# An instance norm on one core: another dealing of row blocks to partitions, and direct emission of the hand-scheduled part

## The chip, the core and the metric

One core of a Trainium2 chip runs the whole kernel. The metric is the device time of one execution in microseconds (us), as a median over runs. TensorE is not used. The work is done by VectorE (DVE), ScalarE (ACT) and the core's sixteen DMA engines. SyncE (SP) only waits and issues transfers.

## What is computed

The input is a float32 array of 256 batches, 256 channels and 4096 positions, thus 65,536 rows of 4096 values. Each row is normalised by its own mean and variance:

```
mean = np.mean(x, axis=2, keepdims=True)
var = np.var(x, axis=2, keepdims=True)
return ((x - mean) / np.sqrt(var + eps)).astype(np.float32)
```

Every row is independent of every other, so any row may be worked on in any partition, as long as its result is written back to where it came from. The input holds 1073.7 MB and the output as much. Each byte is read once and written once.

## The kernel before

**Tiling.** The 65,536 rows are cut into 128 tiles of 512 consecutive rows (8 MB). `x_t` and `out_t` (lines 34 and 35) give the layout within a tile: partition p of the 128 holds the K = 4 consecutive rows 4p to 4p+3. Four rows of 4096 float32 values are 64 KB, which lie next to each other in HBM. So a tile is 128 blocks of 64 KB; partition p holds block p, and the blocks of neighbouring partitions are neighbours in HBM.

**Buffers.** Three SBUF buffers `X[0]` to `X[2]` of 128 x 4 x 4096 take the tiles in turn. A tile is normalised in place and stored from the same buffer.

**Work on a tile.** For each of the four rows in a partition, VectorE makes one pass that scales and sums (line 87). ScalarE then squares and sums the deviation from the mean (line 137) and takes the root (line 146). VectorE makes the reciprocal and the offset (lines 98 and 100). The final scaling is VectorE's (line 112) except for three quarters of the last row, which ScalarE does (line 151). Both engines run these as a loop over tiles written out for three buffers (lines 225 and 237), with a few tiles before and after.

**Transfers.** All loads and stores are issued by SyncE, on one queue, in an order written out by hand (lines 196 to 218). In the loop of line 208 each step is `store(t)` (line 165), then `load(t + 2)` (line 170). The store waits for the five done marks of its tile; the load waits for the store of tile t - 1, since it takes that buffer. Waits and clears are the helper `take` (lines 66 to 68). The first and the last tile move in two halves (lines 199 and 181), so that the compute starts and ends earlier. The function `rows_of` (line 155) picks a tile's rows in HBM, by a constant number outside the loop and by the loop's register inside it.

**Emission.** The three programs are written in `nc.Block()`, with one function for each engine (lines 193 to 246). At its end the block brings the engines together (line 193).

## Time and profile before

| what | value |
|---|---|
| median of ten runs | 4962.64 us (4961.6 to 4999.17; nine of them at or below 4963.14) |
| the profiled execution's own time | 4963.37 us |
| its span in the profile | 4961.2 us |
| DVE busy | 3297.8 us |
| ACT busy | 2407.6 us |
| HBM read, written | 1073.74 MB, 1073.74 MB |
| DMA issues | 259, of them 253 of 8 MB and 6 of 4 MB |

The profiled execution's time and its span differ by 2.2 us, which lie outside the span. A sum over the trace is a sum against 4961.2 us of span; the profiled execution lies 0.7 us above the median. Besides the groups of instructions, the trace has a record of each packet that a DMA engine moved (start, duration, bytes), without the engine's number. All but a few of these packets are one partition's share of a tile, 64 KB.

### The profile page before, as it was taken

To read this page: it belongs to the slowest core of one execution; us is meant where nothing else is said; L and a number is where in the kernel's file an instruction comes from. 1 tells how busy PE (TensorE), PEld (TensorE's weight loads), DVE (VectorE), ACT (ScalarE), POOL (GpSimd) and SP (SyncE) were. 2 spreads that over 40 slices of the span, in tenths; PEclk is the share of its full clock that TensorE was granted. 3 is DMA by queue.
4 is the path that set the end of the run, shared out by engine and by line. 5 is a ranking of instruction groups with operands and counts; after the bars stand their busy time and mean duration, and the time that the engine had idled before them with its cause. 6 is when DMAs were issued, how large, how long until landed. Compare 5 with 4: busy or idle time off the path is not lost.

```text
span 4961.2 us, 5954 instructions
## 1 busy us (share of the span) xinstructions
DVE 3297.8 (66%) x2049; ACT 2407.6 (49%) x1412; POOL 0.2 (0%) x4
## 2 busy tenths in 40 slices
DVE  6666666666666666666666666666666666666666
ACT  4455444554445544455445544455444554445544
POOL 0000000000000000000000000000000000000000
DMA  9999999999999999999999999999999999999999
GB/s 422 431 437 431 434 434 432 436 434 432 438 432 432 437 433 434 435 433 436 433 433 436 433 432 437 433 433 435 433 436 433 433 436 434 432 437 433 433 436 398
DMA packets 37298, 2147.52 MB, mean 433 GB/s; under 512 B 4144, under 2 KB 4144, under 8 KB 4144
## 3 DMA queue, kind: packets, MB, share of 16 engines
q1 hardware_dynamic: 37296, 2147.50, 100.0%
q14 instruction: 2, 0.02, 0.0%
HBM read 1073.74 MB, written 1073.74 MB: 433 GB/s over the span
## 4 chain that ended last, share of the span: by engine, by line
DVE 62%; another core or an unknown queue 31%; issue 4%; DMA 2%; ACT 0%; DVEq 0%; ACTq 0%; SPq 0%
DVE x L87 44%; DVE x L112 16%; DMA x<-in_x_dram 1%; DVE nbias L100 1%; DMA out_dram<-x 1%; DVE rstd L98 1%; ACT junk L137 0%; DVEq L68 0%; DVEq L225 0%; ACT L146 0%; ACT std L146 0%; DVEq L193 0%; ACTq L68 0%; ACTq L67 0%
## 5 line engine op out<-in xcount | busy, mean ns | idle before, releaser
L87 DVE TENSOR_SCALAR_CACHE_REDUCE x<-x 128x4096 f32<-128x4096 f32 x512 | 2232.3, 4416 | 1581.3 <-DMA x<-in_x_dram 1581.3
L137 ACT ACTIVATE junk<-x,mean 128x4096 f32<-128x4096 f32 x512 | 1883.1, 3678 | 2368.2 <-DVE x L87 2368.2
L112 DVE TENSOR_SCALAR x<-x,rstd,nbias 128x4096 f32<-128x4096 f32 (+1 forms) x512 | 1004.1, 2003 | 33.9 <-DVE nbias L100 29.3
L151 ACT ACTIVATE x<-x,nbias,rstd 128x3072 f32<-128x3072 f32 x130 | 383.1, 2947 | 146.0 <-DVEq L68 146.0
L137 ACT ACTIVATION_READ_ACCUMULATOR junk<-x,mean 128x1 f32 x512 | 95.5, 186 | 0.0
L146 ACT ACTIVATE std<-ss,eps_tile 128x2 f32<-128x2 f32 x256 | 75.6, 295 | 19.1
L98 DVE RECIPROCAL rstd<-std 128x2 f32<-128x2 f32 x256 | 40.6, 158 | 19.4 <-ACT std L146 19.4
L100 DVE SCALAR_TENSOR_TENSOR nbias<-mean,rstd 128x2 f32<-128x2 f32 x256 | 41.0, 160 | 8.9
L87 DVE DVE_READ_ACCUMULATOR x<-x 128x1 f32 x512 | 42.3, 83 | 0.0
L137 ACT ACT_TABLE_LOAD x1 | 1.3, 1283 | 1.2 <-DVE eps_tile L222 1.2
L146 ACT ACT_TABLE_LOAD x1 | 1.3, 1283 | 0.1
L222 DVE MEMSET eps_tile<- 128x1 f32 x1 | 0.1, 59 | 1.0 <-SPq L192 1.0
L259 POOL MEMSET const-bfloat16-1.0<- 128x1 bf16 x1 | 0.1, 101 | 0.0
L259 POOL MEMSET const-uint8-127<- 128x1 uint8 x1 | 0.1, 101 | 0.0
L259 POOL MEMSET const-float32-0.0<- 128x1 f32 x1 | 0.1, 99 | 0.2 <-issue 0.2
L259 POOL MEMSET const-float32-1.0<- 128x1 f32 x1 | 0.1, 98 | 0.0
## 6 DMA issues: line engine op xcount, KB each, us to landing
out_dram<-x SPq DMA_DIRECT2D x4, 4096.0 KB, 19.5
x<-in_x_dram SPq DMA_DIRECT2D x2, 4096.0 KB, 16.7
x<-in_x_dram SPq DMA_DIRECT2D x127, 50.3
out_dram<-x SPq DMA_DIRECT2D x126, 31.6
```

The source lines that it names most:

```text
L87: V.tensor_scalar(out=x[:, r, :], in0=x[:, r, :], scalar1=1.0 / d, scalar2=None, op0=ALU.mult, op1=ALU.add, accum_out=mean[s][:, r : r + 1 ...
L98: mine(V.reciprocal(out=rstd[s][:, c], in_=std[s][:, c]))
L100: mine(V.scalar_tensor_tensor(out=nbias[s][:, c], in0=mean[s][:, c], scalar=-1.0 / d, in1=rstd[s][:, c], op0=ALU.mult, op1=ALU.mult))
L112: V.tensor_scalar(out=x[:, r, f], in0=x[:, r, f], scalar1=rstd[s][:, c], scalar2=nbias[s][:, c], op0=ALU.mult, op1=ALU.add,).then_inc(dn, 1)
L137: mine(A.activation(out=junk, in_=x[:, r, :], func=AF.Square, bias=mean[s][:, c], scale=-float(d), accum_out=ss[s][:, c]))
L146: A.activation(out=std[s][:, c], in_=ss[s][:, c], func=AF.Sqrt, bias=eps_tile, scale=1.0 / d**3).then_inc(stds, 1)
L151: A.activation(out=x[:, last, :Q], in_=x[:, last, :Q], func=AF.Identity, bias=nbias[s][:, c], scale=rstd[s][:, c]).then_inc(dn, 1)
L222: V.memset(eps_tile, eps / d**2).then_inc(ready, 1)
L259: nc = _bacc.Bacc("TRN2", target_bir_lowering=False, num_devices=1)
```

## The change

The first part takes the three programs out of `nc.Block()` and its functions, and emits the same calls one after the other inside `tc.tile_critical()`. The instructions on VectorE, ScalarE and SyncE keep their order; only branches into and out of the block and the block's closing synchronisation differ.

The second part changes which rows of a tile go to which partition. Before, block b of the 128 blocks of a tile goes to partition b. Now the block number is written b = 16 j + e, with j from 0 to 7 and e from 0 to 15, and block b goes to partition 8 e + j. Loads and stores both use the new order, so the output is the same. The tile size, the number of transfers, the 64 KB in one piece and all compute instructions stay as they are. The HBM side of a transfer was 128 entries of 64 KB (step 64 KB). It is now 16 entries (step 64 KB), each of 8 pieces (step 1 MB) of 64 KB. The SBUF side is 128 partitions as before.

```diff
+    E = 16
-    x_t = x_flat.rearrange("(t p k) d -> t p k d", p=P, k=K)
-    out_t = out_flat.rearrange("(t p k) d -> t p k d", p=P, k=K)
+    x_t = x_flat.rearrange("(t j e k) d -> t e j k d", e=E, k=K, j=P // E)
+    out_t = out_flat.rearrange("(t j e k) d -> t e j k d", e=E, k=K, j=P // E)
...
-        return ap[bass.ds(i, 1)].rearrange("o p k d -> p (o k) d")
+        return ap[bass.ds(i, 1)].rearrange("o e j k d -> e (o j) k d")
...
-        S.dma_start(out=out_t[t][:, r, :], in_=X[s][:, r, :]).then_inc(second(stored, s, h), 16)
+        S.dma_start(out=out_t[t][:, :, r, :], in_=X[s][:, r, :]).then_inc(second(stored, s, h), 16)
...
     with tc.tile_critical():
-        with nc.Block() as block:
-
-            @block.sync
-            def _(sync):
-                for h in range(2):
-                    r = half_of(h)
-                    S.dma_start(out=X[0][:, r, :], in_=x_t[0][:, r, :]).then_inc(second(loaded, 0, h), 16)
-                load(1, 1, wait=False)
...
-            @block.vector
-            def _(vector):
-                V.memset(eps_tile, eps / d**2).then_inc(ready, 1)
...
-            @block.scalar
-            def _(scalar):
-                take(A, ready, 1)
...
+        for h in range(2):
+            r = half_of(h)
+            S.dma_start(out=X[0][:, r, :], in_=x_t[0][:, :, r, :]).then_inc(second(loaded, 0, h), 16)
+        load(1, 1, wait=False)
...
+        V.memset(eps_tile, eps / d**2).then_inc(ready, 1)
...
+        take(A, ready, 1)
```

## Prediction

> **What bounds the kernel now.** I read the page's shares and its rows by slice first, then its queues.

> ```profile
> DVE 3297.8 (66%) x2049; ACT 2407.6 (49%) x1412; POOL 0.2 (0%) x4
> DMA  9999999999999999999999999999999999999999
> GB/s 422 431 437 431 434 434 432 436 434 432 438 432 432 437 433 434 435 433 436 433 433 436 433 432 437 433 433 435 433 436 433 433 436 434 432 437 433 433 436 398
> q1 hardware_dynamic: 37296, 2147.50, 100.0%
> ```

> No compute engine is busy for more than two thirds of the span, while the DMA engines are busy in every slice. The table by stretch (columns: DVE, ACT and POOL busy, PEclk, DMA share, GB/s) says how full they are, in the middle and at the end.

> ```profile
> 1000.00:2000.00 1000.00, 665.83 (x415) 483.21 (x283) 0.00 (x0) 1.00 1.00 434
> 3000.00:4000.00 1000.00, 665.53 (x415) 483.08 (x283) 0.00 (x0) 1.00 1.00 434
> 4940.00:4961.00 21.00, 2.26 (x2) 2.10 (x1) 0.00 (x0) 1.00 0.57 245
> ```

> In the middle the share is 1.00 at 434 GB/s. Only the end is slack. Next, the groups of instructions: what does DVE wait for ahead of its first pass over a tile?

> ```profile
> L87 DVE TENSOR_SCALAR_CACHE_REDUCE x<-x 128x4096 f32<-128x4096 f32 x512 | 2232.3, 4416 | 1581.3 <-DMA x<-in_x_dram 1581.3
> ```

> For loads, 1581.3 us in all. The chain of waits names DVE for 62%, because SP waits for DVE before each store; that is not the bound, as the order of SP's issues and the times to landing show.

> ```profile
> 1004.54 0.35 SPq L170 DMA_DIRECT2D x<-in_x_dram  x1
> 1042.79 0.34 SPq L165 DMA_DIRECT2D out_dram<-x  x1
> ```
> ```profile
> x<-in_x_dram SPq DMA_DIRECT2D x127, 50.3
> ```

> The load issued at 1004.54 lands about 50.3 us later, at 1054.8. The next store is issued at 1042.79, when some 12.0 us of that load are still to be moved. The engines therefore never run dry. From the first to the last of 78 load issues between 1004.54 and 3980.01 us there are 77 tiles, (3980.01 - 1004.54) / 77 = 38.642 us each, for 16.777 MB in and out: 434.2 GB/s. 128 tiles of that are 4946.2 us, so 15.0 us of the span are ends.

> The packet records say what each engine does in this time: 30,937 of 32,384 packets of 64 KB took exactly 2418 ns (27.1 GB/s), and only 117 took over 2500. A tile is 16 packets per engine, 8 in and 8 out: 38.642 / 16 = 2.415 us each. Each engine runs at a fixed rate of its own, back to back, and HBM isn't seen to slow it. So nearness in HBM has nothing to win here; the question is whether the new dealing keeps each engine at 2.415 us.

> [...]

> [...]

> [...]

> [...]

> **The change part by part.** *Direct emission.* It drops a few branches and the block's closing synchronisation (L193). At the start the first load is issued at 0.96 us; at the end the last store is taken note of at 4959.8 us and the span ends at 4961.2. L193's part of these 1.4 us is 0.3 us. Between -0.5 and +0.5 us; I take 0. The orders on the engines are unchanged, so no DMA passes another and no wait is added.

> *Issue of a three-dimensional pattern.* An issue takes 0.34 us (L165) or 0.35 (L170); how long for the new pattern is not shown. It might be nothing more, or double. 259 issues x 0.35 us = 91 us if nothing hid it, but the 12.0 us of queued transfer do; only the first issues are exposed, under 1 us. I take 0.

> *Packets.* 64 KB in one piece as before, 8 in and 8 out per engine and tile. Compute is the same: DVE's 25.8 us per tile (3297.8 / 128) stay beneath the transfer.

> *The split over engines.* This is the step that counts. The HBM side has only 16 outer entries, each with the blocks of eight adjacent partitions. [...] with sixteen engines, one entry each, an engine has partitions 8e to 8e+7. [...] it is my inference. [...]

> How much of it is met depends on the lead w (in packets) of one engine of a pair over the other: of four packets the leader has w alone, and 4 - w at half rate, so that a stretch takes (8 - w)/4 of its old time. w = 0 is twice, w = 4 is no loss. [...] The first sixteen packets of the run start within 0.72 us of one another by their records, 0.72 / 2.418 = 0.3 packet. I take w = 0.3: factor 1.925, 38.642 x 1.925 = 74.39 us per tile. 128 x 74.39 = 9521 us, plus 15.0 of ends is a span of 9536, plus the 2.2 us that lie outside the span (4963.37 - 4961.2), less 0.7 for profiled execution against median: 9538 us. With w = 0 it is 128 x 77.28 + 16.5 = 9909. The unknown cost itself is bounded by 0 (the pair out of step[...]) and by +4946 us (all in step).

> **The rivals.** *Only one direction shares, or a middling lead.* [...] With one side free, a tile is 19.32 + 38.64 = 57.96 us: 7436 us (7200 with the lead of 0.3). A lead of two packets gives 1.5 and the same time. For it: nothing in the trace has shown contention of either kind. [...]

> *Not slower: the pairs fall out of step.* If a pair shares unfairly, its lead grows; from w = 4 packets, 9.7 us, [...] the loss is gone. The 12.0 us of queued work would just allow such a lead. For it: 109 of the 117 packets over 2500 ns lie before 1060 us, so the engines do settle into a pattern without collisions in this kernel. It would end at 4960 us. [...] Against: a lead of four packets must come from somewhere, where 0.3 is what the start gives.

> *HBM order hurts.* [...] Blocks that sixteen engines take side by side have a pitch of only 64 KB, so I hold it for unlikely.

> *Faster.* [...] over 0.3% is all but excluded.

> **How the numbers follow.** Pairs in step both ways (9300 to 9950): 0.61. One direction or a middling lead (7200 to 9300): 0.19. Hidden (4945 to 4976): 0.16. HBM order (5000 to 7200): 0.03. Faster: 0.01. The range from 7200 to 9950 leaves out the last three, 0.20. The nine close runs of the kernel before lie within 0.03%; 0.3% is about what can be told from no change. Faster 0.01, same 0.16, slower 0.83. The time is that of the likeliest case, 9538 us.

> **What would show it.** If right: packet records of mostly some 4.8 us instead of 2.418 with a DMA share still near 1.00, some 225 GB/s in the stretches, about 74 us between load issues, DVE's wait for loads grown to some 6100 us with its busy time at 3298. Stores at 2.4 us beside loads at 4.8 us would be the first rival. [...] A DMA share well under 1.00 would mean late issues, which I have put at nothing.

## The result, and the profile after

The changed kernel takes 9121.99 us, a median of 9 runs (9080.56 to 9172.69), beside 4962.56 us before, a median of 30. The ratio is 1.8372, with a 95% interval of 1.8333 to 1.8411. Here and below, medians are of all runs of a kernel, while ratios rest on its fast runs alone, those at most 1.5% above its fastest, so that the two need not divide out. The forecast was 9538 us with a range from 7200 to 9950: the side is right, the packets are slower at a full busy share as it said, and the likeliest time is 416 us (4.6%) too high. The forecast rested on the author's estimate that the engines come in pairs, that the two of a pair have half the rate each while they are in step, and that such steps are four packets long. No trace of the kernel before shows any of this.

First the shares and the queue on the page of the changed kernel.

```profile
DVE 3298.1 (36%) x2049; ACT 2407.6 (26%) x1412; POOL 0.2 (0%) x4
DMA  9999999999999999999999999999999999999998
q1 hardware_dynamic: 37296, 2147.50, 99.7%
```

Number of packets, bytes and engine work are as before, and the DMA engines are still busy in every slice. The busy time of DVE differs by 0.3 us. What changed is what a busy DMA engine gets done; the table by stretch, with the same columns as before:

```profile
1000.00:2000.00 1000.00, 361.04 (x224) 262.40 (x154) 0.00 (x0) 1.00 1.00 235
3000.00:4000.00 1000.00, 361.02 (x224) 262.41 (x154) 0.00 (x0) 1.00 1.00 234
```

The share is still 1.00, at 234 to 235 GB/s instead of 434. So a busy share of 1.00 doesn't tell how fast the packets move: it stood beside 434 GB/s before and stands beside 234 now. DVE's wait ahead of its first pass takes up the difference:

```profile
L89 DVE TENSOR_SCALAR_CACHE_REDUCE x<-x 128x4096 f32<-128x4096 f32 x512 | 2232.3, 4416 | 5741.1 <-DMA x<-in_x_dram 5741.1
```

It grew by 4160 us, and the median of the kernel by 4159. The order of SP's issues, from 3000 to 3150 us:

```profile
3043.82 0.57 SPq L167 DMA_DIRECT2D out_dram<-x  x1
3050.19 0.60 SPq L172 DMA_DIRECT2D x<-in_x_dram  x1
3115.76 0.56 SPq L167 DMA_DIRECT2D out_dram<-x  x1
3122.15 0.60 SPq L172 DMA_DIRECT2D x<-in_x_dram  x1
```

Two things are to be seen. An issue takes 0.57 and 0.60 us instead of 0.34 and 0.35. And the load now follows its store by 6.4 us, where it was 0.6: it waits for the store of the tile before, which lands later. SP's waits for stores, before and after:

```profile
SPq L68 <- DMA out_dram<-x: 47.7, 3, 30.7
SPq L70 <- DMA out_dram<-x: 820.5, 128, 70.7
```

That is 820.5 / 128 = 6.4 us each, on average. From 1046.1 to 8989.9 us there are 112 load issues, (8989.9 - 1046.1) / 111 = 71.57 us per tile.

The packet records show where this comes from. Besides the 64 KB packets they hold, before and after, 768 of 32 KB (the tiles in halves) and 4,144 of 4 bytes, as many as 16 engines times 259 transfers. Of 32,384 packets of 64 KB, before 30,937 took 2418 ns; now 7.6% take less than 2500 ns, 67% more than 4600, and 56% lie between 4880 and 5400; the mean of all is 4466. This is no uniform slowing: some packets move at the old rate and most at about half of it.

### The profile page after: what moved, and what is told of

The parts are those of the page before. It is cut to its first block, busy times and chain, and to the rows that moved or that the text cites. A ratio compares the mean times of both kernels' runs of the same rounds, so it can differ in the third digit from the quotient of the medians.

```text
span 9164.9 us, 5938 instructions
## 1 busy us (share of the span) xinstructions
DVE 3298.1 (36%) x2049; ACT 2407.6 (26%) x1412; POOL 0.2 (0%) x4
## 2 busy tenths in 40 slices
DMA packets 37298, 2147.52 MB, mean 234 GB/s; under 512 B 4144, under 2 KB 4144, under 8 KB 4144
## 3 DMA queue, kind: packets, MB, share of 16 engines
q1 hardware_dynamic: 37296, 2147.50, 99.7%
## 4 chain that ended last, share of the span: by engine, by line
another core or an unknown queue 62%; DVE 34%; issue 2%; DMA 0%; ACT 0%; DVEq 0%; SPq 0%; ACTq 0%
DVE x L89 24%; DVE x L114 9%; DVE nbias L102 1%; DMA x<-in_x_dram 0%; DVE rstd L100 0%; ACT junk L139 0%; DVEq L70 0%; DVEq L221 0%; ACT std L148 0%; SPq L197 0%; ACTq L70 0%; ACTq L69 0%; SPq L267 0%; SPq L194 0%
## 5 line engine op out<-in xcount | busy, mean ns | idle before, releaser
L89 DVE TENSOR_SCALAR_CACHE_REDUCE x<-x 128x4096 f32<-128x4096 f32 x512 | 2232.3, 4416 | 5741.1 <-DMA x<-in_x_dram 5741.1
```

The costliest lines, as they stand in the source:

```text
L89: V.tensor_scalar(out=x[:, r, :], in0=x[:, r, :], scalar1=1.0 / d, scalar2=None, op0=ALU.mult, op1=ALU.add, accum_out=mean[s][:, r : r + 1 ...
```

## The experiments

**e1_direct_only.** The emission alone:

```diff
-    x_t = x_flat.rearrange("(t j e k) d -> t e j k d", e=E, k=K, j=P // E)
-    out_t = out_flat.rearrange("(t j e k) d -> t e j k d", e=E, k=K, j=P // E)
+    x_t = x_flat.rearrange("(t p k) d -> t p k d", p=P, k=K)
+    out_t = out_flat.rearrange("(t p k) d -> t p k d", p=P, k=K)
...
```

> The direct emission alone, with the old dealing of rows. Port theory [...]: nothing but the block's closing step goes, 4962 us within 1 us. Rival, the emission has a part in the loss: clearly over 4975, up to 9122.

4962.21 us, ratio 0.9993 (0.9979 to 1.0007). The emission costs and saves nothing that can be measured.

**e2_dealing_only.** The converse: the kernel before, with nothing changed but its layout.

```diff
-    x_t = x_flat.rearrange("(t p k) d -> t p k d", p=P, k=K)
-    out_t = out_flat.rearrange("(t p k) d -> t p k d", p=P, k=K)
+    x_t = x_flat.rearrange("(t j e k) d -> t e j k d", e=E, k=K, j=P // E)
+    out_t = out_flat.rearrange("(t j e k) d -> t e j k d", e=E, k=K, j=P // E)
...
```

> The new dealing alone, in the old block with a program per engine. Port theory: the whole loss, 9122 (9050 to 9180). Rival, the two parts only cost together: nearer 4962.

9169.34 us, ratio 1.8465 (1.8426 to 1.8504), on another chip than e1. The dealing alone brings the whole loss. That its ratio lies 0.5% above the changed kernel's is not explained.

**e3_near_by_port.** Entries of four partitions instead of eight:

```diff
-    E = 16
+    E = 32
```

> The changed kernel with E = 32 instead of 16: partition 4q + j holds block 32 j + q, so the HBM side is 32 entries of 4 pieces. [...] Port theory: packets of 2418 ns again and 4962 us (4955 to 4975), although the pattern has three dimensions and its issue takes 0.57 to 0.60 us as in the changed kernel. Rival, neighbouring blocks in HBM hurt each other: about 9100. Rival, the three-dimensional pattern itself is slow on the queue: about 9100.

4962.27 us, ratio 0.9999 (0.9991 to 1.0007). One number takes the loss away, with the step of 64 KB from entry to entry and the three-dimensional pattern kept. Its table by stretch:

```profile
1000.00:2000.00 1000.00, 666.01 (x414) 483.22 (x283) 0.00 (x0) 1.00 1.00 434
```

And its issues of loads, in the list of the line's instructions (min/median/max in ns):

```profile
L172 SPq DMA_DIRECT2D x<-in_x_dram x127: 592/607/639, 2.3 to 4862.2; - x127
```

The issue takes as long as in the changed kernel, and 434 GB/s are back. So the rival of the three-dimensional pattern falls, and the 0.25 us more per issue are shown to be hidden. How the 32 entries are dealt to the engines is not shown. Dealt two by two in their order, they would give an engine partitions 8e to 8e + 7 again, and by the theory the loss; the return of the rate speaks against that. Entries on neighbouring blocks are thus no cause of the loss by themselves; the next run tests the HBM rival from the other side.

**e4_apart_by_entry.** Sixteen entries, but 1 MB apart in HBM, each with its eight blocks in a row (SyncE's loop is written out for it):

```diff
-    x_t = x_flat.rearrange("(t j e k) d -> t e j k d", e=E, k=K, j=P // E)
+    x_p = x_flat.rearrange("(t e u j k) d -> t u e j k d", e=E, u=2, k=K, j=P // E)
+    x_t = [x_p[t // 2, t % 2] for t in range(ntiles)]
...
-        with S.Fori(0, rounds) as i:
-            for t in range(L0, L0 + BUFS):
-                store(t % BUFS, (t, BUFS, rounds, i))
-                load((t + 2) % BUFS, (t + 2, BUFS, rounds, i))
+        for t in range(L0, last - 2):
+            store(t % BUFS, t)
+            load((t + 2) % BUFS, t + 2)
```

> The changed kernel's 16 entries of 8 pieces, but each entry's eight blocks follow one another in HBM and the entries are 1 MB apart (two tiles share a stretch of 16 MB), [...] SyncE's loop is written out. Port theory: the split by whole entries is the same, so 9122 again (9000 to 9250). Rival, HBM order: about 4962.

9084.17 us, ratio 1.8315 (1.8287 to 1.8343). The order in HBM is the opposite, the loss the same. One order could still lose by chance what the other loses; the next run has the old order and loses too, and with that the HBM rival is out.

**e7_two_partition_halves.** The old dealing and two-dimensional patterns, every transfer in two halves of the partitions (built on e1):

```diff
+    groups = (slice(0, 64), slice(64, 128))
...
-        S.dma_start(out=X[s][:, :, :], in_=rows_of(x_t, t)).then_inc(loaded[s], 16)
+        for g in groups:
+            S.dma_start(out=X[s][g, :, :], in_=rows_of(x_t, t)[g]).then_inc(loaded[s], 16)
...
-            take(V, ld, 16)
+            take(V, ld, 32)
...
```

> The old dealing and the old two-dimensional pattern, but every transfer in two: partitions 0 to 63 and then 64 to 127. HBM order stays as before, and each engine still gets 64 KB pieces, 4 and 4. Port theory: [...] about 9100 (8300 to 9900). HBM rival and the rival of the three-dimensional pattern: about 4962, at most 60 us more for the issues.

9093.92 us, ratio 1.8363 (1.8313 to 1.8413). This kernel shares neither the order of blocks nor the pattern with the changed one, and has the same loss: 236 GB/s against 234 to 235. So neither the new order nor the third dimension is needed for it; transfers of 64 partitions each bring it too. It is the strongest of the runs against the rivals. That the two kernels lose by one and the same collision was the author's supposition; their ratios, 1.8363 and 1.8372, agree with it, and nothing in the records shows it directly.

```profile
1000.00:2000.00 1000.00, 363.06 (x226) 264.13 (x155) 0.00 (x0) 1.00 1.00 236
```

The packet records of the changed kernel hold a sign of groups of four. A packet starts within some 20 ns of the end of the one before it on its engine, and a 4-byte record closes each engine's share of a transfer. So 1,400 of the 4,048 shares of eight 64 KB packets can be followed with never a second candidate. Of their first to eighth packets 51, 40, 2, 19, 23, 2, 1 and 18% took under 4000 ns (in e2 49, 40, 2, 20, 22, 2, 1 and 18%). Short packets are commonest at both ends of each group of four. That fits engines which meet on a group of four partitions and of which one goes on to the next group earlier than the other. It is a reading of the records, which don't tell what is shared.

**e5_loads_by_entry and e6_stores_by_entry.** One direction alone. In e5 only `out_t` goes back to the old layout, in e6 only `x_t`:

```diff
-    out_t = out_flat.rearrange("(t j e k) d -> t e j k d", e=E, k=K, j=P // E)
+    out_t = out_flat.rearrange("(t p k) d -> t p k d", p=P, k=K)
...
```

> Loads with the new dealing, stores with the old one; the output's 64 KB blocks stand in another order within a tile, so part of the computation (where rows are written) is changed. Theory that both directions share ports alike: half of the loss stays, (4962 + 9122) / 2 = 7042 us (6800 to 7300). Rival, writes into SBUF share and reads don't: the whole loss, about 9100. Rival, reads only: 4962.

> The converse: loads with the old dealing, stores with the new one; again the output's blocks stand in another order within a tile. Both directions alike: 7042 us (6800 to 7300). Writes only: 4962. Reads only: about 9100.

7545.55 us (7338 to 7591) and 6952.77 us (6538 to 6992). Since only one side of a tile is dealt anew, both kernels write rows to other places than they should. Each direction alone costs time. Over the 4963.61 us of the kernel before, loads cost 2582 us by the median and 2374 by the fastest run, stores 1989 and 1574. The sums, 4571 and 3948, lie on either side of the 4159 of the changed kernel. Loads cost more in both readings, so "alike" was not right: all runs of e5 lie outside its 6800 to 7300, and the fastest of e6 does too.

The engines' shares of transfers that can be followed in the two profiles (7591 and 6967 us) form two groups. In e5, 673 shares have packets with a mean of 4922 ns and 692 one of 2457; in e6, 336 have 4166 and 566 have 2516. The slow group is presumably the direction dealt anew. Its first packet took under 4000 ns in 6% of the shares of e5 and in 98% of those of e6. By the theory much of the difference thus lies in a longer time alone; that a slowed store is cheaper than a slowed load is not shown.

**e9_halves_by_entry and e10_extra_work_for_a_lead.** These test what the forecast said of leads. e9 moves each tile in two halves of the partitions, each with 16 entries of 4 blocks:

```diff
-    x_t = x_flat.rearrange("(t j e k) d -> t e j k d", e=E, k=K, j=P // E)
+    x_t = x_flat.rearrange("(t g j e k) d -> t g e j k d", g=2, e=E, k=K, j=P // E // 2)
...
-        S.dma_start(out=X[s][:, :, :], in_=rows_of(x_t, t)).then_inc(loaded[s], 16)
+        for g in range(2):
+            S.dma_start(out=X[s][64 * g : 64 * g + 64, :, :], in_=rows_of(x_t, t)[g]).then_inc(loaded[s], 16)
...
```

e10 adds to e9 one transfer of 32 blocks ahead of the loop, meant to give one engine of each pair four packets more. Its page has eight 4-byte packets more than that of e9 (8,296 against 8,288), so eight engines had a share of it; which ones is not shown.

```diff
         load(0, 3)
+        rows = slice((ntiles - 1) * P * K, (ntiles - 1) * P * K + 128)
+        S.dma_start(
+            out=out_flat[rows].rearrange("(j e k) d -> e j k d", e=8, j=4),
+            in_=x_flat[rows].rearrange("(j e k) d -> e j k d", e=8, j=4),
+        ).then_inc(extra, 16)
...
```

> Two transfers per tile, partitions 0 to 63 and 64 to 127, each with an HBM side of 16 entries of 4 blocks: [...] It is the ground for the next run. Port theory: [...] about 9100 (8900 to 9300). If only the changed kernel's own order of blocks were slow: other than that, towards 4962.

> The run before plus one transfer at the start [...] four packets of 64 KB each from HBM to HBM, into rows that the last tile overwrites. [...] Theory that a pair only loses while in step and that a lead is kept: [...] 4975 to 5600 us, with most packets at 2418 ns, although there is more work. Theory that ports or halves are slow whatever the phase: some 10 us more than the run before. If leads die away: a fast start and then packets of about 5 us, between 5600 and 9100.

8966.15 us (8800 to 9161) for e9 and 8936.31 us (8886 to 9034) for e10, ratio of the latter 1.7999 (1.7886 to 1.8111). The two can't be told apart by their times, and e10 is far from 4975 to 5600, so the case that leads are kept failed. Whether the lead died away or never did anything is told by the tables by stretch. First e9, then e10:

```profile
100.00:200.00 100.00, 36.25 (x26) 27.46 (x17) 0.00 (x0) 1.00 1.01 239
200.00:250.00 50.00, 18.27 (x11) 12.42 (x8) 0.00 (x0) 1.00 1.01 263
250.00:300.00 50.00, 7.52 (x6) 6.33 (x4) 0.00 (x0) 1.00 0.99 260
300.00:400.00 100.00, 48.09 (x28) 34.53 (x21) 0.00 (x0) 1.00 0.97 239
400.00:600.00 200.00, 62.90 (x40) 43.80 (x24) 0.00 (x0) 1.00 1.00 238
```
```profile
100.00:200.00 100.00, 35.38 (x26) 26.60 (x17) 0.00 (x0) 1.00 1.01 244
200.00:250.00 50.00, 24.51 (x15) 17.63 (x11) 0.00 (x0) 1.00 0.99 295
250.00:300.00 50.00, 13.44 (x7) 8.22 (x4) 0.00 (x0) 1.00 1.00 319
300.00:400.00 100.00, 39.63 (x29) 30.39 (x20) 0.00 (x0) 1.00 0.92 303
400.00:600.00 200.00, 82.69 (x51) 57.31 (x34) 0.00 (x0) 1.00 0.99 266
600.00:800.00 200.00, 72.36 (x47) 55.16 (x33) 0.00 (x0) 1.00 0.98 251
1000.00:2000.00 1000.00, 380.41 (x235) 275.92 (x162) 0.00 (x0) 1.00 1.00 241
```

The extra transfer is issued at 116 us, behind other queued ones. Part of the jump that follows is there without it: e9 rises to 263 GB/s and is back at 239 after 300 us. With it, with more to do for some engines, the rate reaches 319 GB/s and still has 303 from 300 to 400 us. Then the gain dies away; from 1000 us on the rate is 241, against 240 in e9. A share of 0.92 at 300 to 400 us says that some engines ran dry there, but the rate goes on falling at shares of 0.98 and 0.99. What brings the loss back wasn't settled.

**e8_row_halves and e11_alternating_ports.** If a pair has a small lead all the same, what counts by the theory is how long an engine stays on one group of four partitions. e8 halves that stay, with two transfers of two rows each (and packets of 32 KB):

```diff
-        S.dma_start(out=X[s][:, :, :], in_=rows_of(x_t, t)).then_inc(loaded[s], 16)
+        for h in range(2):
+            r = half_of(h)
+            S.dma_start(out=X[s][:, r, :], in_=rows_of(x_t, t)[:, :, r, :]).then_inc(loaded[s], 16)
...
```

e11 quarters it: it has four transfers over every fourth partition, so that two blocks of an entry in one transfer lie four partitions apart. Each block is in its partition as in the changed kernel:

```diff
-    x_t = x_flat.rearrange("(t j e k) d -> t e j k d", e=E, k=K, j=P // E)
+    x_t = x_flat.rearrange("(t a g e k) d -> t g e a k d", a=2, g=4, e=E, k=K)
...
-        S.dma_start(out=X[s][:, :, :], in_=rows_of(x_t, t)).then_inc(loaded[s], 16)
+        for g in range(4):
+            S.dma_start(out=X[s][g:P:4, :, :], in_=rows_of(x_t, t)[g]).then_inc(loaded[s], 16)
...
```

> The changed kernel with every transfer in two row halves, [...] If a pair keeps a lead that is fixed in time (0.65 packets of 64 KB by the factor 1.837 = (8 - 0.65) / 4), the factor falls to (4 - 0.65) / 2 = 1.675, 8300 us. If pairs settle at the same share of a run, or a run's length doesn't matter: 9122 as before.

> The changed kernel's dealing of blocks, but each transfer in four, over the partitions g, g + 4, g + 8 and so on (g from 0 to 3), [...] Lead fixed in time at 0.65 packets: factor 2 - 0.65 = 1.35, 6700 us. Run length doesn't matter: about 9100. A pair that trips over itself once and then alternates out of step: about 4965, with packets of 2418 ns.

6871.57 us, ratio 1.379 (1.371 to 1.387), and 5255.58 us (5149 to 5347), ratio 1.0425 (1.0377 to 1.0474). Both are faster than the time that a lead of 0.65 packets gives (8300 and 6700 us), and far from "run length doesn't matter". e11 comes nearest to its third case, a pair that trips over itself and then alternates, about 4965 us. Its table by stretch:

```profile
0.00:120.00 120.00, 50.30 (x33) 43.00 (x25) 0.20 (x4) 1.00 1.00 253
120.00:240.00 120.00, 67.00 (x39) 47.60 (x28) 0.00 (x0) 1.00 0.99 380
240.00:400.00 160.00, 104.91 (x65) 76.56 (x46) 0.00 (x0) 1.00 1.00 425
1000.00:2000.00 1000.00, 645.13 (x401) 468.76 (x276) 0.00 (x0) 1.00 1.00 424
3000.00:4000.00 1000.00, 605.10 (x373) 438.04 (x256) 0.00 (x0) 1.00 1.00 393
```

With every block in the same partition as in the changed kernel and by the theory the same split over engines, another order of the partitions brought 393 to 425 GB/s instead of 234. It starts at 253 GB/s and recovers within 240 us. In the terms of the theory the pairs fall out of step by themselves here, so that a lead can grow as well as die away. More and smaller transfers are hardly the reason, since e7 and e9 had two for each tile and kept the loss; four with the long stays were not run.

How large would the lead be, if a packet in step is charged with what the records show instead of twice 2.418 us? The 56% between 4880 and 5400 ns have a mean of 5.06 us, which is 2.09 times 2.418. With L packets of 64 KB per stay and a lead of w, L x ratio = (L - w) x 2.09 + w:

| kernel | L | ratio | w in packets of 64 KB |
|---|---|---|---|
| after | 4 | 1.837 | 0.93 |
| e8 | 2 | 1.379 | 1.30 |
| e11 | 1 | 1.0425 | 0.96 |

These are estimates, worked out from the ratios and that mean, and the model is a rough one. At L = 1 a lead of 1 is all that counts, so e11 can't tell one packet from more. And 0.93 would give e8 a ratio of 1.58 where 1.379 was measured. In the shares that could be followed, the first four packets were also shorter than the second four (means of 4307 and 4752 ns), so the lead isn't one number. What is left is an estimate of its size, about one packet of some 2.4 us.

## Why the prediction was right

*The bound.* Right: at a share of 1.00 on all engines, every loss of rate went straight into the time (DVE's wait +4160 us, median +4159).

*Direct emission, 0 us.* Right: e1.

*Three-dimensional issue, 0 us.* Right, although an issue takes 0.23 to 0.25 us more. No part of it that can be measured is on the path: e3 issues at 0.607 us and ends at 4962.27. The cover is what the forecast named, the transfers queued ahead.

*The split over engines.* The step that counts, and an inference when it was made. Four runs agree with it: 32 entries restore the rate (434 GB/s, e3), 16 entries lose it with the opposite order in HBM too (237 to 240, e4), halves of the partitions lose it without entries (236 to 241, e7), and the order of the partitions alone brings most of it back (393 to 425, e11). The short packets at the ends of each group of four fit it as well. What the runs show is which cuts of a tile lose here (16 entries of 8 partitions, halves of 64 partitions), and that the loss lies in the duration of packets. That engines meet in pairs, and on what, was the author's estimate and is still not shown.

*The factor.* The term that was mis-sized. The forecast had (8 - 0.3)/4 = 1.925 and the runs 1.837. By the estimate above both parts of it were off, in opposite directions: a packet in step takes some 5.06 us and not 4.84, which alone would give more; and the lead is about one packet and not 0.3, which gives less, and this is the greater of the two. That the time came within 4.6% is in part luck: with 5.06 us and a lead of 0.3 the factor would be (3.7 x 2.09 + 0.3) / 4 = 2.01 and the time some 9960 us, at the very end of the range (9950). For the same reason +4946 us, twice the old packet, was no upper bound. The 0.3 supposed that the start decides, and that failed: in e10 a gain died away, from 319 to 241 GB/s, and in e11 one came by itself, from 253 to 425, so a lead, if it is one, does change, and 0.3 was a value without ground. The rival of a pair that stays out of step didn't come true for long stays, although e10 reached 319 GB/s for a while, and e11 came near the old rate.

*A sum.* For one direction with a lead of 0.3 the forecast has 7200 us. By its own terms it is 128 x 38.642 x (1 + 1.925) / 2 + 16.5 = 7250 us. Nothing hangs on it.

*The signs that were named.* Per tile 71.57 us (about 74 forecast), 234 to 235 GB/s (225), DVE's wait 5741 us (6100), slow packets of 4.88 to 5.4 us (4.8). The first three are off by 3 to 6%, all towards a smaller loss; the packets are off the other way. The rival of one direction falls by e5 and e6, the HBM rival by e3, e4 and e7. The 5000 to 7200 us that the forecast gave to the HBM rival were the author's estimate, and no run shows such a cost.

*What e3 offers.* It has the aim of the change, neighbouring blocks in neighbouring entries, without the loss, and is equal to the kernel before (0.9991 to 1.0007). The order in HBM won nothing over the kernel before with its 2418 ns per packet, as the forecast had said.

## What to carry to other kernels

When a transfer's HBM side is reshaped, ask how its outer entries group the partitions, not only whether all sixteen engines are in use: here 16 outer entries of 8 partitions ran at 234 GB/s and 32 entries of 4 at 434, with the same bytes, packets and busy share. In a kernel whose DMA share is 1.00, look at the duration of single packets: here a uniform 2418 ns left nothing to win from the order in memory (e3, 0.9999) and something to lose. If entries of eight partitions can't be avoided, try transfers over every fourth partition: here they lost much less (1.04 instead of 1.84).

## What the runs showed of the hardware that was not expected

- The slow packets of the changed kernel, those of 4880 to 5400 ns, have a mean of 5.06 us. An estimate, if two engines move such packets side by side: 2 x 65,536 B / 5.06 us = 25.9 GB/s together, less than the 27.1 GB/s of one packet in 2.418 us.
- Loads and stores both take part, and loads dealt by entry cost more than stores: 2582 us against 1989 by the medians (e5, e6).
- A gain from extra work for some engines doesn't last: 319 GB/s at 250 to 300 us where e9 has 260, and 241 after 1000 us (e10). With four transfers over every fourth partition one comes by itself: 253 GB/s at the start and 425 after 240 us (e11).
- SP takes 0.55 to 0.61 us (medians in the changed kernel, e3 and e4) to issue a transfer with a three-dimensional pattern over 128 partitions, against 0.34 to 0.35 us for a two-dimensional one. The number of dimensions is not all of it: in e7 a two-dimensional one over 64 partitions took 0.53 us.
